# A planner's table of matmul durations is set to the spacings seen in the trace, and all operations are ordered anew

## The chip, the core and the metric

The kernel runs on one core of a Trainium2 chip. The metric is the device time of one execution in microseconds. A core has five engines that run side by side: PE (TensorE, the matrix engine, whose weight loads are listed apart as PEld), DVE (VectorE), ACT (ScalarE), POOL (GpSimd) and SP (SyncE, which issues the DMA transfers of this kernel). Each engine takes its own instructions in the order of the program, and waits where one of them needs a result of another engine or of a transfer.

## What is computed

One layer of a hybrid decoder, for a prompt of 512 tokens and for 8 samples of one token each, with D = 1024 and shared weights. The 512 + 8 = 520 tokens go through the products together. Cut to what matters:

```
mod = silu(c) @ w_ada + b_ada             # shift, scale, gate, twice
h = rmsnorm(x) * (1 + scale) + shift
proj = h @ w_in                           # u | z | xBC | dt | g_a | g_b
ya = S5(u)                                # 64 groups x 64 complex states, scan over time, gelu, half-GLU
yb = SSD(z, conv(xBC), dt)                # 32 heads of 64, d_state 128, chunks of 128 tokens
merged = sigmoid(g_a) * (ya @ w_branch_s5) + sigmoid(g_b) * (yb @ w_branch_ssd)
x += gate * rmsnorm(merged @ w_out)
x += gate_f * rmsnorm(swiglu(modulate(rmsnorm(x)) @ w_ffn_in) @ w_ffn_out)
```

The outputs are x for both groups and the new states: S5, SSD and convolution, for the prompt and for each sample.

## The kernel before, in words

Features lie on partitions, tokens along the free axis, in two halves of 260. All large products run as three matmuls with fp32r operands: weight and input are each split into a high and a low part, and high x high, high x low and low x high are summed (`product`, line 1148). For one block of 128 features by 128 and two halves of tokens that makes six matmuls of 260 columns, which are one operation of the **main stream**. The weights come in tiles of 512 KB by DMA; ACT makes their high part (`whi`, line 696) and DVE the low part (`wlo`, line 640). A finished tile in a PSUM bank pair (`pm`) is evacuated by ACT or DVE.

Beside the main stream run **side works**, written as generators: the modulation from `w_as` and `w_ada`, the eight S5 units (`s5_prep`, `s5_load`, `s5_body`, whose data go through DRAM as `ud`, `kd` and `yd` to change their layout), sixteen SSD units (`ssd_unit`, which load a broadcast row `acd` each), the samples' outputs (`ssd_y`, from `in_ssmT`) and the samples' new states (`ssd_state`, line 2369). This last one is a loop of 32 steps over two buffers: a load of 256 KB (`in_ssm`), three DVE operations on 512 columns, a store of 256 KB (`out_ssm_s`); the next load into a buffer waits for its store. Small matmuls of side works write to single banks (`bank`).

The order of all this is not written by hand. Every helper (`vtt`, `act`, `dma`, `mm`, ...) only records an operation, with the memory that it touches and an estimate of its duration, and a planner orders the records:

- While recording, `add` (line 240) gives each operation a time at once. `main` (line 755) moves the clock `now` on by the cost of a main product, and `tick` (line 823) lets side works record as much as fits before `now`. Memory is given out in this pass too.
- `order` (line 275) gives each operation a priority: for the main stream a running sum of its costs times `MAINF` = 1.1 (line 287), for side works the longest way to a main product or to the end. Then `play` (line 352) runs a course in which each engine takes the most urgent operation that can start, and `back` (line 315) derives new priorities from that course played backwards. This repeats 7 times, and then 24 times more with some priorities shifted at random (`SEED` = 149), three courses each. The course whose planned end is earliest becomes the program: the instructions of each engine in that order.
- `play` and `back` take the duration of an operation from the estimate of its helper, and the delay between engines from a table `DELAY` (line 179). For a transfer `dma` (line 698) takes 0.475 us (or 0.65) for the issue, 0.65 us, the bytes at 360 GB/s, and `DELAY` then adds 0.907 us to a reader on DVE; the transfers of the first weights, of `in_w_as` and of x have fixed urgencies from 1999 downward. The estimates for DVE are `.068 + columns / 960` us for two tensors (line 640), for ACT `.052 + columns / 1200` and a little more.

The planner acts when the program is built, not on the chip. Lines of the rows below are those of the helpers: L722 is every matmul of `mm`, L734 every transpose of `tp`, L729 the matmuls on zeros, L640 `vtt`, L696 `acp`, L691 `act`, L712 the DMA issue.

Of the kernel before, what the change touches and what calls it, by code (L numbers as in the profile page):

```python
# [49 lines left out]
class Root:  # L50
    """A tile: `get` gives the real one (it may be made late); `loc` names the memory it lies in."""
# [14 lines left out]
class Ap:  # L66
    """A view of a tile: its shape and addresses at once, the real view when the operation is issued."""
# [65 lines left out]
    def cells(self):  # L133
        """Partitions, and the set of words in one of them (bits of an integer)."""
        if self.root.bank:
            return 0, 128, 1
        p0, col = divmod(self.off, PSTEP)
        pn, run, outer = 1, 1, []
        for s, n in sorted(self.dims):
            if s >= PSTEP:  # L140
                pn = n
            elif s and n > 1:
                if s <= run:
                    run += s * (n - 1)
                else:
                    outer.append((s, n))
        m = (1 << run) - 1
        for s, n in outer:
            b = m
            for i in range(1, n):  # L150
                m |= b << (i * s)
        return p0, p0 + pn, m << col


def fold(dims):
    """The dimensions with neighbours joined where one stride serves both."""
    out = []
    for s, n in reversed(dims):
        if out and s == out[0][0] * out[0][1]:
            out[0] = (out[0][0], n * out[0][1])  # L160
        else:
            out.insert(0, (s, n))
    return out
# [14 lines left out]
# delay in us from the end of an operation to the start of one that waits for it  # L178
# [7 lines left out]
class Line:  # L186
    """The time of one engine: busy stretches, into whose gaps operations are put."""
# [24 lines left out]
class Plan:  # L212
    """Records operations with the memory they touch, and orders them for the engines."""
# [51 lines left out]
    def remake(self, loc, fn, words):  # L265
        """The memory `loc` gets a new tile: after everything that used the old one."""
        h = self.hist.get(loc, [])
        deps = {e[4]: .2 for e in h}
        o = Op("X", 0.0, fn, deps, None, 0.0)
        o.n = len(self.ops)  # L270
        self.ops.append(o)
        o.start = o.fin = max((p.fin for p in deps), default=0.0)
        self.hist[loc] = [[0, 128, (1 << words) - 1, True, o]]

    def order(self):
        """The best of some schedules: by the longest way to the end, then by latest starts."""
# [6 lines left out]
        after = 0.0  # L283
# [31 lines left out]
    def back(self):  # L315
        """Priorities from the schedule played backwards: the time from an operation's latest start to the end."""
# [35 lines left out]
    def play(self):  # L352
        """The course of the operations, each engine taking the most urgent of those that can start."""
# [69 lines left out]
    def shift(self, t, free, cand):  # L423
        """An operation of DVE that ACT may take at time t, where that is done sooner."""
# [32 lines left out]
class Arena:  # L457
    """One run of words in a tile of one type; blocks are cut out of it first fit."""
# [39 lines left out]
class Mem:  # L498
    """A fixed float32 arena, and slots whose type (float32 or float32r) is chosen when one is empty."""
# [10 lines left out]
    def find(self, n, dt, top):  # L510
        """The place for n words: an arena index (0 = the fixed one), or None."""
        if n > SLOT or (top or self.low and dt == F32) and self.a0.fit(n):
            return 0 if self.a0.fit(n) else None
        part = [(s.words(), i) for i, s in enumerate(self.slots) if self.mode[i] == dt and s.fit(n)]
        if part:
            return min(part)[1] + 1
        if dt == F32 and self.a0.fit(n) and n < 1500:
            return 0
        for i in range(NSLOT):
            if self.mode[i] is None:  # L520
                return i + 1
        if dt == F32 and self.a0.fit(n):
            return 0
        return None
# [76 lines left out]
class Builder:  # L601
# [76 lines left out]
    def relu(self, o, a, s):  # L678
        """max(a + s, 0)"""
# [18 lines left out]
    def dma(self, o, a, boost=0.0):  # L698
        """Starts a transfer; returns the estimate of its end."""
# [16 lines left out]
    def mm(self, o, l, r, start=True, stop=True):  # L716
        n, m = self.fs(r), l.shape[-1]
        if l.dtype == F32R:
            c = max(n / 2400, .111) if m > 32 else .048
        else:  # L720
            c = max(n * 4 / 2400, .216) * max(m, 32) / 128 + (.021 if m <= 64 else 0.0)
# [3 lines left out]
    def idle(self, o, n, after=None):  # L725
        """Matmuls on zeros."""
# [5 lines left out]
    def tp(self, o, a, n):  # L732
        d = self.ident[:n, :n]
        self.pe(.108, lambda: self.nc.tensor.transpose(real(o), real(a), real(d)), [o], [a, d])  # L734
# [8 lines left out]
    def bunch(self):  # L743
        """Matmuls that have to follow one another (sums that are open in one bank)."""
# [10 lines left out]
    def main(self):  # L755
        """The matmuls gathered in `group`, as one operation of the main stream."""
# [24 lines left out]
    def can(self, sizes, dt=F32, spare=0):  # L781
        """Whether the blocks fit, with room for `spare` token rows beside them."""
# [13 lines left out]
    def wblk(self, sizes, spare=2, dt=F32, prio=2):  # L796
        """Blocks for side work; a request that waits holds back those of less urgent work."""
# [88 lines left out]
    def ahead(self, j, table, f):  # L886
        """Prepares the weights of the use j of a chunk, unless that is done."""
# [12 lines left out]
    def build(self):  # L900
# [27 lines left out]
        # weight stream  # L928
# [30 lines left out]
        # half of the tokens at a time where the next step waits for all features  # L959
# [15 lines left out]
        # startup: modulation for the mixer, first norm  # L975
# [36 lines left out]
        # the first three tiles advance with the scale, two feature blocks at a time  # L1012
        b23 = [self.banks.pop() for _ in range(2)]
        ps = [[self.pm[0][:, n] for n in both], [self.pm[1][:, n] for n in both], b23]
        if NDUM:
            # matmuls on zeros: they keep the array busy, and so its clock at the full rate, until there are data
# [127 lines left out]
    def span(self, n):  # L1144
        """The tokens of half n."""
        return slice(n * self.cutp, n * T + (1 - n) * self.cutp)

    def product(self, hi, lo, k, p, halves, start, stop, xh, xl):
        """One block of features in a tile of the main stream."""
# [11 lines left out]
    def dt_mm(self, k, p, w):  # L1161
        """The 32 columns of dt, high and low parts side by side, summed later."""
# [50 lines left out]
    def scaled(self, k):  # L1213
        """hi/lo of the scaled input, a feature block: not yet normalized, and without the shift."""
# [11 lines left out]
    def evac_u(self, i, p):  # L1226
        """A tile of u made from the scaled input: normalized here."""
# [6 lines left out]
    def shift(self, gens):  # L1234
        """The shift; what it adds to the tiles of u that were made without it."""
# [31 lines left out]
    def turn(self, p, ev, n, md):  # L1267
        """Sums the four parts of sums in p, feature to partition."""
# [12 lines left out]
    def shifted(self, k):  # L1281
        """hi/lo of the normalized, scaled and shifted input."""
# [13 lines left out]
    def ada_s(self, k):  # L1296
        """The scale of the mixer's input, a feature block."""
# [52 lines left out]
    def ada_last(self):  # L1350
        """The gate of the second branch, in small pieces: needed much later, so it fills gaps."""
# [24 lines left out]
    def evac(self, kind, i, p, halves):  # L1376
# [9 lines left out]
        elif kind == "dt":  # L1386
            # the weights' high and low parts; later a chunk (and two samples) of a head a partition
# [136 lines left out]
    def cols(ap, halves):  # L1524
        """The tokens of the halves."""
# [35 lines left out]
    def mix_in(self, i, n, pv):  # L1561
        """A tile of the branch, times its gate and weight, and its squares, for half n of the tokens."""
# [58 lines left out]
    def finish(self, n):  # L1621
# [6 lines left out]
        for k in range(KD):  # L1628
            m, x, o = self.mixk(k)[:, c], self.xrk(k)[:, c], self.O["y"]
            self.vtt(m, m, rs, MULT)  # L1630
            if k < len(xp):
                # this sum on the tensor engine
# [12 lines left out]
    def rstd_last(self):  # L1645
        """The reciprocal deviations of the last 256 tokens: made with a token a partition, then spread by matmuls."""
# [39 lines left out]
    def gated(self):  # L1686
        # squares, normalization and splits of the SSD branch
# [43 lines left out]
    def s5(self):  # L1731
# [45 lines left out]
        # f = (abar - 1) / lam  # L1777
# [18 lines left out]
        # unit rotation by 8 angles  # L1796
# [30 lines left out]
        # powers in falling order, for B: the steps of a chunk that are left after a token  # L1827
# [39 lines left out]
    def ring(self, key, q, n, sizes):  # L1867
        """Blocks of the n-deep ring `key` for unit q; taken when first needed."""
# [10 lines left out]
    def s5_tabs(self, unit):  # L1879
        """cos and (signed) sin of 8 c theta, c = 0 .. 63, for the 8 groups of a unit, by doubling."""  # L1880
# [4 lines left out]
        for q in range(0, 8, 2):  # L1885
            w, pb = yield from self.ring("tw", 0, 1, [512, 1536])
            # planes: -sin, cos, sin; 64 partitions for each of the two units
# [35 lines left out]
    def s5_prep(self, q, un, KP, BB32):  # L1923
# [14 lines left out]
        # f B and, in bb's first plane, its copy; f B with its parts exchanged  # L1938
# [54 lines left out]
    def s5_load(self, q, un, U, Hm):  # L1993
# [18 lines left out]
        # decay of a chunk; the step of the samples' states  # L2012
# [81 lines left out]
    def ssd(self):  # L2094
# [25 lines left out]
        # dt = softplus(raw + bias)  # L2120
# [32 lines left out]
        # minus the sums of a; decay to chunk end times dt  # L2153
# [45 lines left out]
    def ssd_group(self, g, acd, act, dtT, ddT):  # L2199
        BT, CT = self.bt[g].v(T), self.ct_[g].v(T)  # L2200
        bs_, Bs, CB = yield from self.wblk([128, 512, 512], 0, F32, 1)
        # the samples: rows of B, columns of C, products for their dot products
# [44 lines left out]
    def ssd_unit(self, m, bl, Bs, CB, CT, acd, act, dtT, ddT, end):  # L2247
        """Two heads (one tile of 128 features): chunk states, recurrence over chunks, output, gate."""
# [72 lines left out]
    def ssd_y(self):  # L2321
        """The samples' outputs: C on the decayed old states (n on the partitions here), C B on what the new token adds."""
# [46 lines left out]
    def ssd_state(self):  # L2369
        """The samples' new states, a feature a partition."""  # L2370
# [31 lines left out]
def layout(inputs):  # L2402
# [18 lines left out]
    # S5 features: channel before group within a tile  # L2421
# [82 lines left out]
```

## Time and profile before

| | |
|---|---|
| time, three runs | 1200.11, 1202.06, 1204.35 us; median 1202.06 us |
| profiled execution | span 1193.2 us from the first to the last instruction; its own time is recorded by that span alone, 8.9 us below the median |
| PE busy | 1168.8 us, 98% of the span, 10,182 matmuls |
| PEld busy | 1124.5 us, 94% |
| DVE busy | 814.7 us, 68% |
| ACT busy | 576.3 us, 48% |
| DMA | 195.49 MB, 164 GB/s on average |
| granted TensorE clock | 0.998 of full speed on average |

Busy time of an engine is the union of its instructions. Matmuls overlap in the pipeline: one of 260 columns is shown with about 283 ns while the next one starts some 120 ns after it, so that the time per matmul is read from how many start in a stretch and not from the duration of one. A stretch without idle time of PE is one where no stop shows in its stream.

### The profile page before, as it was taken

Reading aid. Unit: us, or ns where it says so; the run is one execution under the profiler, and the core shown is the slowest. Engines: PE = TensorE matmul, PEld = TensorE weight load, DVE = VectorE, ACT = ScalarE, POOL = GpSimd, SP = SyncE. Lnnn points to the kernel's source line nnn. Section 1 sums busy time; section 2 is a strip of 40 time slices with the busy share of each in tenths; the row PEclk is TensorE's granted clock in tenths of the full one; section 3 lists DMA queues with packets and bytes.
Section 4 is the critical chain, followed back from the end, with each engine's and each line's share of the span. In section 5 each row is a group of like instructions: output and inputs, shape, how many; then the busy total and the mean of one; then the engine's idle time right before and its main releaser. Section 6 shows DMA issues by size and latency. Waiting matters only on the chain.

```text
span 1193.2 us, 24814 instructions
## 1 busy us (share of the span) xinstructions
PE 1168.8 (98%) x10182; PEld 1124.5 (94%) x10182; DVE 814.7 (68%) x1651; ACT 576.3 (48%) x981; POOL 4.9 (0%) x32
## 2 busy tenths in 40 slices
PE   8999999999999999999999999999999899999998
PEld 6899898999999999999998989999999899999997
DVE  6898989997696877868885435499576673322236
ACT  6655444357487657847853323465223222222233
POOL 0000000000000000000000000000000000000000
PEclk9999999999999999999999999999999999999999
DMA  8838698667243343355545674344566663223244
GB/s 292 278 119 219 162 215 224 180 160 208 82 134 101 114 128 125 116 175 169 188 145 201 241 268 144 129 166 147 182 217 203 198 206 104 88 81 97 83 130 135
DMA packets 118066, 195.49 MB, mean 164 GB/s; under 512 B 45856, under 2 KB 68800, under 8 KB 115648
## 3 DMA queue, kind: packets, MB, share of 16 engines
q1 hardware_dynamic: 117952, 193.90, 52.9%
q8 instruction: 80, 1.31, 0.4%
q14 instruction: 34, 0.28, 0.1%
HBM read 165.81 MB, written 23.86 MB: 159 GB/s over the span
## 4 chain that ended last, share of the span: by engine, by line
PE 79%; DMA 9%; DVE 7%; issue 1%; SPq 1%; ACT 1%; DVEq 0%; ACTq 0%
PE pm L722 64%; PE bank L722 14%; DVE s L640 4%; DMA arena<-in_ssm 3%; DVE arena L640 2%; PE bank L734 2%; DMA s<-in_w_as 1%; DMA out_ssm_s<-arena 1%; SPq L712 1%; DVE wlo L640 1%; DMA s<-in_w_in 1%; DMA ud<-s 1%; DMA s<-s 1%; DVE s L663 1%; ACT s L696 0%
## 5 line engine op out<-in xcount | busy, mean ns | idle before, releaser
L722 PE MATMUL pm<-hi,whi 128*128 128x260 f32 (+1 forms) x1856 | 497.5, 289 | 5.9 <-DVE arena L640 3.7
L722 PE MATMUL pm<-lo,whi 128*128 128x260 f32 (+1 forms) x1856 | 483.4, 282 | 0.0
L722 PE MATMUL pm<-hi,wlo 128*128 128x260 f32 x1840 | 370.4, 283 | 0.0
L722 PEld LDWEIGHTS pm<-hi,whi 128*128 128x128 f32 (+1 forms) x1856 | 349.6, 188 | 17.4 <-issue 13.0
L722 PEld LDWEIGHTS pm<-lo,whi 128*128 128x128 f32 (+1 forms) x1856 | 349.1, 188 | 0.1
L640 DVE TENSOR_TENSOR wlo<-arena,whi 128x1024 fp32r<-128x1024 f32 (+1 forms) x157 | 188.8, 1203 | 146.7 <-ACT whi L696 144.9
L722 PEld LDWEIGHTS pm<-hi,wlo 128*128 128x128 f32 x1840 | 282.9, 188 | 0.0
L696 ACT CAST whi<-arena 128x1024 fp32r<-128x1024 f32 (+1 forms) x158 | 162.6, 1029 | 197.1 <-PE pm L722 180.2
L722 PE MATMUL pm<-s,whi 128*128 128x260 f32 (+2 forms) x1128 | 184.2, 283 | 0.0
L640 DVE TENSOR_TENSOR arena<-arena 128x512 f32<-128x512 f32 (+11 forms) x299 | 140.3, 494 | 49.8 <-DMA arena<-in_ssm 29.4
L722 PEld LDWEIGHTS pm<-s,whi 128*128 128x128 f32 x1128 | 156.2, 188 | 5.1 <-issue 4.2
L722 PE MATMUL pm<-s,wlo 128*128 128x260 f32 (+2 forms) x564 | 117.2, 283 | 0.0
L722 PEld LDWEIGHTS pm<-s,wlo 128*128 128x128 f32 x564 | 88.1, 188 | 0.0
L691 ACT ACT_TABLE_LOAD x63 | 80.8, 1283 | 10.3 <-DMA s<-acd 3.5
L722 PE MATMUL bank<-s,s 128*64 128x128 f32 (+5 forms) x672 | 75.8, 282 | 5.6 <-ACT s L696 4.4
L722 PEld LDWEIGHTS bank<-s,s 128*128 128x128 f32 (+2 forms) x672 | 61.3, 164 | 10.9 <-ACT s L696 5.3
L691 ACT ACTIVATE s<-s 128x520 f32<-128x520 f32 (+10 forms) x89 | 50.0, 570 | 38.3 <-DVE s L640 17.7
L691 ACT ACTIVATE arena<-pm 128x260 f32<-128x260 f32 (+3 forms) x44 | 21.2, 489 | 92.7 <-PE pm L722 85.7
L640 DVE TENSOR_TENSOR s<-arena,s 128x520 fp32r<-128x520 f32 (+5 forms) x60 | 56.5, 948 | 10.6 <-ACT s L696 10.4
L640 DVE TENSOR_TENSOR s<-s,arena 128x8 f32<-128x8 f32 (+6 forms) x138 | 48.6, 369 | 13.8 <-ACT s L691 12.7
L722 PE MATMUL bank<-hi,s 128*128 128x260 f32 x256 | 55.5, 285 | 0.0
L722 PE MATMUL pm<-hi,s 128*128 128x260 f32 x256 | 55.0, 285 | 0.0
(122 smaller groups left out, 1265.8 us busy)
## 6 DMA issues: line engine op xcount, KB each, us to landing
arena<-in_w_in SPq DMA_DIRECT2D x59, 512.0 KB, 3.7
arena<-in_w_fi SPq DMA_DIRECT2D x44, 512.0 KB, 4.4
arena<-in_w_ada SPq DMA_DIRECT2D x12, 1024.0 KB, 7.5
arena<-in_w_fo SPq DMA_DIRECT2D x20, 512.0 KB, 3.6
arena<-in_ssmT SPq DMA_DIRECT2D x16, 512.0 KB, 4.4
s<-acd SPq DMA_DIRECT2D x16, 512.0 KB, 4.3
arena<-in_w_bssd SPq DMA_DIRECT2D x16, 512.0 KB, 5.4
arena<-in_ssm SPq DMA_DIRECT2D x32, 256.0 KB, 3.8
```

Of the source, the lines that this page charges most:

```text
L640: self.op("V", .068 + self.fs(o) / 960, lambda: self.nc.vector.tensor_tensor(out=real(o), in0=real(a), in1=real(b), op=op), [o], [a, b, *a ...
L663: self.op("V", .068 + self.fs(o) / 960, lambda: self.nc.vector.tensor_tensor_scan(out=real(o), data0=real(a), data1=real(b), initial=0.0, ...
L691: self.op("A", c, lambda: self.nc.scalar.activation(real(o), real(a), f, bias=real(bias), scale=real(scale)), [o], [a, scale, bias], None ...
L696: self.op("A", c, lambda: self.nc.scalar.copy(real(o), real(a)), [o], [a])
L712: p = self.op("S", .475 if same else .65, lambda: self.nc.sync.dma_start(out=real(o), in_=real(a)), [o], [a], None, c)
L722: self.pe(c, lambda: self.nc.tensor.matmul(real(o), lhsT=real(l), rhs=real(r), start=start, stop=stop), [o], [l, r])
L734: self.pe(.108, lambda: self.nc.tensor.transpose(real(o), real(a), real(d)), [o], [a, d])
```

## The change

Three estimates of PE's durations get other values, in microseconds; n is the number of columns of the moving operand, m that of the stationary one. Comments and docstrings go as well, which leaves blank lines (the line numbers stay). Nothing else differs in the file, but as the planner orders by these numbers, the recording, the use of memory and the order of all engines can come out different.

```diff
     def mm(self, o, l, r, start=True, stop=True):
         n, m = self.fs(r), l.shape[-1]
         if l.dtype == F32R:
-            c = max(n / 2400, .111) if m > 32 else .048
+            c = max(n / 2400 + (.0114 if n < 300 else .0025), .112)
         else:
-            c = max(n * 4 / 2400, .216) * max(m, 32) / 128 + (.021 if m <= 64 else 0.0)
+            c = max(n * 4 / 2400 + .005, .224) * max(m, 32) / 128 + (.021 if m <= 64 else 0.0)
...
     def tp(self, o, a, n):
         d = self.ident[:n, :n]
-        self.pe(.108, lambda: self.nc.tensor.transpose(real(o), real(a), real(d)), [o], [a, d])
+        self.pe(.112, lambda: self.nc.tensor.transpose(real(o), real(a), real(d)), [o], [a, d])
```

## Rows read from the trace of the kernel before

**Rows 1.** The page: the span, and engines with busy us, share and instructions.

```profile
span 1193.2 us, 24814 instructions
...
PE 1168.8 (98%) x10182; PEld 1124.5 (94%) x10182; DVE 814.7 (68%) x1651; ACT 576.3 (48%) x981; POOL 4.9 (0%) x32
```

**Rows 2.** Stretches: start to end, length, busy us per engine, clock, DMA share, GB/s.

```profile
0.00:42.00 42.00, 35.62 (x332) 28.69 (x333) 26.32 (x96) 25.73 (x63) 1.59 (x11) 1.00 0.92 328
...
90.00:245.00 155.00, 145.94 (x1274) 142.27 (x1273) 139.37 (x286) 72.35 (x172) 1.70 (x15) 0.99 0.80 198
245.00:600.00 355.00, 355.00 (x3328) 343.24 (x3327) 282.88 (x626) 246.19 (x350) 0.39 (x1) 1.00 0.46 141
...
845.00:955.00 110.00, 105.87 (x884) 105.48 (x883) 74.72 (x102) 28.83 (x37) 0.00 (x0) 1.00 0.63 201
955.00:1158.00 203.00, 203.00 (x1695) 203.00 (x1694) 73.60 (x93) 56.38 (x88) 0.00 (x0) 1.00 0.36 111
1158.00:1193.20 35.20, 30.36 (x232) 28.51 (x230) 20.75 (x44) 14.00 (x26) 0.00 (x0) 0.98 0.46 144
```

**Rows 3.** Chain by line: 0 to 60, 90 to 245, 245 to 600, 810 to 890, 890 to 956.

```profile
by line: PE pm L722 34.7%; DMA s<-in_w_as 26.8%; DMA s<-in_w_in 15.6%; SPq L712 8.7%; PE bank L722 7.5%; PE bank L734 1.8%; ACT whi L696 1.7%; issue 1.4%; ACT s L696 0.8%; ACTq L696 0.0%
...
by line: DVE s L640 26.0%; issue 7.1%; PE pm L722 6.5%; DVE wlo L640 6.1%; DVE arena L640 6.0%; DMA ud<-s 5.5%; DMA s<-s 5.1%; SPq L712 4.7%; DVE s L663 4.1%; ACT s L696 3.3%; DMA s<-in_s5m 3.3%; DMA s<-ud 3.0%; DMA acd<-s 2.8%; DMA arena<-
...
by line: PE pm L722 78.2%; PE bank L722 18.6%; PE bank L734 3.2%
...
by line: PE pm L722 77.0%; PE bank L722 22.6%; PE bank L734 0.5%
...
by line: DMA arena<-in_ssm 45.9%; DMA out_ssm_s<-arena 20.9%; DVE arena L640 16.0%; issue 7.5%; DVE wlo L640 3.9%; PE pm L722 2.4%; DVE s L640 2.2%; SPq L712 1.6%
```

**Rows 4.** Groups of instructions by form, PE: count | busy us, mean ns | idle before.

```profile
L722 PE MATMUL pm<-hi,whi 128*128 128x260 f32 x1840 | 493.7, 289 | 5.9 <-DVE arena L640 3.7 <-ACT s L691 1.0 <-ACT s L696 0.8
L722 PE MATMUL pm<-lo,whi 128*128 128x260 f32 x1840 | 479.6, 282 | 0.0
L722 PE MATMUL pm<-hi,wlo 128*128 128x260 f32 x1840 | 370.4, 283 | 0.0
```

**Rows 5.** Waits (us, times, longest), three of 60 to 270, two of 270 to 600.

```profile
ACT s L696 <- DMA ud<-s: 15.2, 6, 6.0
...
ACT s L696 <- DMA s<-s: 11.0, 9, 4.4
ACT s L691 <- DMA s<-in_s5hy: 6.5, 3, 3.1
...
ACT L691 <- DMA s<-acd: 3.5, 1, 3.5
...
DVE s L682 <- DMA s<-acd: 3.1, 4, 1.2
```

**Rows 6.** Tile in_ssm: loads with first and last issue, who waited, us to landing.

```profile
L712 SPq DMA_DIRECT2D arena<-in_ssm x32: 327/333/457, 813.4 to 973.1; - x32
...
  DVE arena L640: 29.4, 16
...
DMA to landing us min/median/max: 2.5/3.8/5.8
```

**Rows 7.** DMA issues: count, KB each, median us to landing.

```profile
s<-acd SPq DMA_DIRECT2D x16, 512.0 KB, 4.3
...
out_ssm_s<-arena SPq DMA_DIRECT2D x32, 256.0 KB, 3.0
```

**Rows 8.** Stretches as in rows 2: the state loop in two parts; 120 to 150.

```profile
813.40:890.00 76.60, 76.60 (x638) 75.39 (x637) 56.61 (x100) 24.02 (x41) 0.00 (x0) 1.00 0.61 196
890.00:956.00 66.00, 61.87 (x515) 61.48 (x515) 44.34 (x60) 17.41 (x22) 0.00 (x0) 1.00 0.64 204
...
120.00:150.00 30.00, 27.12 (x229) 26.41 (x228) 27.50 (x55) 13.77 (x32) 0.23 (x2) 0.94 0.66 161
```

**Rows 9.** Waits over the whole span: us, times, longest.

```profile
ACT whi L696 <- PE pm L722: 180.2, 59, 6.9
```

## The prediction

> **What bounds the kernel now.** I read the page's list of engines first, to see whether one of them fills the span. It does: PE is busy for 1168.8 of 1193.2 us, so only 24.4 us of the span have no matmul in flight [rows 1]. The change moves instructions and neither adds nor removes one, so the 10,182 matmuls stay, and all that it can move is those idle 24.4 us, in either direction.
>
> Then I read the table of stretches to see where the idle time lies, by subtracting PE's busy time from each stretch [rows 2]. It is 6.4 us in the first 42 us, 9.1 us between 90 and 245 us, 4.1 us between 845 and 955 us and 4.8 us after 1158 us; the other four stretches have none.
>
> The chain of waits, cut to stretches, then says what sets the pace in each [rows 3]. From 245 to 600 us and from 810 to 890 us it is PE alone. From 90 to 245 us (the S5 units) PE has 6.5% of it under its main line, and DVE, DMA and ACT have most of the rest. From 890 to 956 us (the samples' SSD states) the loads and stores of the state loop hold 66.8% (45.9 + 20.9) and PE 2.4%. So there are two places where work beside PE is already the slower partner, and both end in stalls of PE.
>
> **What the change does to the plan.** The planner orders by a table. For a product with 260 token columns the old table says 260/2400 = 108.3 ns, the new one 119.7 ns, a factor of 1.105. The chip agrees with the new one: between 955 and 1158 us PE runs 1,695 matmuls, nearly all of that form, in 203.00 us, 119.8 ns each [rows 2]. Three groups of this form alone hold 3 x 1840 = 5,520 of the 10,182 matmuls [rows 4]; at 11.4 ns each they add 63 us to the planned PE time. The durations of DVE, ACT and DMA in the table stay. On the chip PE takes what it took; what changes is how much PE work the plan lays beside a given amount of other work.
>
> That is the step on which the forecast rests. The old plan believed that 108.3 ns of other work fit beside one matmul, and the chip gave it 119.8 ns. So each stretch of other work had about 10% more time on the chip than planned, and late transfers were swallowed by that. The new plan lays only as many matmuls beside it as really fit. Because every engine takes its queue in the planned order, PE then meets a matmul whose input is late earlier than before.
>
> **The terms.** *PE's own work:* 10,182 matmuls before and after, 0 us.
>
> *Start and end:* in the first 60 us loads of w_as hold 26.8% of the chain and those of w_in 15.6% [rows 3]; they are the first transfers issued, by fixed urgencies (1999, then 1990 less their place) that no table touches, so I take 0 for the 6.4 us. The 4.8 us at the end are the last sums and their output, which nothing else can cover: 0 us.
>
> *The S5 stretch, 90 to 245 us:* the chip lays 145.9 us of PE beside this work [rows 2], and the old plan thought of it as 145.9 / 1.105 = 132.1 us. If the new plan lays 132.1 us of real PE time there and the work takes its present 155 us, PE idles 22.9 us, 13.8 us more than now. If the work shrinks to DVE's busy 139.4 us [rows 2], PE idles 7.3 us, 1.8 us less. The lowest end is that all 9.1 us go. Between -1.8 and +13.8 I take a point a third of the way up, +3.4 us: DVE is busy for 90% of the stretch, so that end is the nearer one, but ACT's waits for transfers (15.2 us for ud, 11.0 for s, 6.5 for s5hy between 60 and 270 us) [rows 5] are waits that no table of PE removes.
>
> *The state loop, 813 to 973 us:* 32 loads are issued from 813.4 to 973.1 us, one every 5.15 us, and DVE waits for 16 of them, 29.4 us in all; a load lands 3.8 us after its issue [rows 6], a store 3.0 us after [rows 7]. The planner's formula for a load of 256 KB (line 698: 0.475 for the issue, 0.65, 262144/360e3 = 0.73, and 0.907 to the reader) makes 2.76 us, about 1 us short. From 890 to 956 us, where the loop sets the pace, 61.9 us of PE lie beside it [rows 8]; the new plan lays 61.9 / 1.105 = 56.0 us there, and if the loop can't be quicker PE idles 10.0 us in place of 4.1, +5.9 us. From 813 to 890 us PE sets the pace and could lose up to 76.6 - 76.6 / 1.105 = 7.3 us if 5.15 us a load is the loop's own limit there too [rows 8], and nothing if it isn't. The lowest end is -4.1, the present stall gone. I take half of 5.9, +3.0 us, since half of the loads are waited for.
>
> For the transfer at the root of this term the Trainium skill, DMA: Bandwidth & Descriptors, section Anatomy of one DMA, gives about 2.0 us fixed plus the bytes at 436 GB/s (a fit for DMAs issued by GpSimd), 2.6 us for 256 KB as an estimate; by that the planner's 2.76 us would be long enough, this term would be 0 and the sum 3.4 us. The trace does not agree: its median is 3.8 us, and the term stands.
>
> *Stretches without idle time, 245 to 845 and 955 to 1158 us:* PE covers all the rest there, so 0 us; what it costs if that cover is gone is the last rival.
>
> *The clock:* one stall in the S5 stretch let the granted clock fall from the 2.4 to the 1.2 GHz level, 0.94 on average from 120 to 150 us [rows 8], which is 0.06 x 30 = 1.8 us of PE time. One more such fall is in the range, not in the sum.
>
> Sum: 0 + 3.4 + 3.0 = +6.4 us. The profiled execution has a span of 1193.2 us, and the median of the three runs, 1202.06 us, is 8.9 us above it for what lies around; I leave that as it is: 1193.2 + 6.4 + 8.9 = **1208.5 us**.
>
> **The rivals.** *Faster: the right table removes the stalls.* Where the old plan expects PE too early, ACT and DVE stand before an evacuation or a free buffer while other work lies behind it in their queues: ACT's split of weights alone waits 180.2 us for PE [rows 9]. An order with the right times fills that, and the S5 work and the loop come earlier. It decides if the transfers named above have work in front of them in the new order. At most the two inner stalls go, 9.1 + 4.1 = 13.2 us; two thirds of that give 1193.3 us. Against it: an ACT that waits for PE marks a place where PE is late, and there PE has no idle time to win.
>
> *No difference.* PE is busy for 98% and every order issues the same matmuls; the first pass of the planner already multiplies main products by MAINF = 1.1, which makes 119.2 ns of 108.3. Then the shuffling of orders (24 perturbations, best by the planner's own end) trades one small stall for another: 1202 us within 3.6. Against it: MAINF stands in the first priorities alone; the course that is played and its reversal use the table's value. Those 3.6 us, 0.3%, are about what a measurement of this kernel can tell from no change.
>
> *Slower in a new place: the SSD units lose their cover.* From 245 to 600 us PE never idles [rows 2], but 16 units each begin with a load of acd that lands after 4.3 us [rows 7], where the planner's formula makes 3.5 us for 512 KB. If each unit's first matmul stands where the plan says, PE waits 0.8 us 16 times, 12.8 us: with the two terms above 1221.3 us, alone 1214.9 us. Against it: DVE has 72 us to spare there [rows 2], and only 3.5 + 3.1 us of waits for acd show on any engine [rows 5].
>
> **How the numbers follow.** The forecast, the lost cover in the two known places, has 0.40. The SSD units' stall has 0.15, no difference 0.21, the removed stalls 0.24. The ends of the terms are 1202.1 - 13.2 = 1188.9 and, with 13.8 + 5.9 + 7.3 + 1.8 = 28.8, 1230.9 us. Leaving out a tenth at each side, the range is 1195 to 1224 us. Faster by over 0.3% has 0.24, within it 0.21, slower 0.55 (0.40 + 0.15). As most of the chance lies on one side, the forecast's own range is 1204 to 1222 us.
>
> **What would show it.** Right: PE idle between 90 and 245 us (or where the S5 units then end) near 12.5 us, and in the state loop near 7 us; the loop's 32 loads in fewer than 160 us of PE work, with DVE's wait for them above 29.4 us; other stretches still without idle time; the same 119.8 ns a matmul. Wrong: less PE idle than 24.4 us in all, which is the first rival; or idle time between 245 and 600 us behind acd or ssmT, which is the last. If the clock falls below 1.00 in more slices than now, the size is wrong and not the mechanism. If the matmul count or the spacing moved, the premise would be wrong.

## The result, and the profile after

The changed kernel takes 1214.74 us (median of 4 runs, 1210.26 to 1218.05) against 1201.09 us before (4 runs, 1198.45 to 1204.35): a ratio of 1.0117, 95% interval 1.0088 to 1.0146. It is slower by 13.7 us; 6.4 us were forecast (1208.5 us, range 1195 to 1224).

The page of the changed kernel, its span and its engines:

```profile
span 1211.3 us, 24833 instructions
...
PE 1181.6 (98%) x10182; PEld 1132.3 (93%) x10182; DVE 811.0 (67%) x1631; ACT 573.3 (47%) x997; POOL 4.7 (0%) x32
```

As many matmuls as in [rows 1], and PE is still busy for 98%. Its idle time is 1211.3 - 1181.6 = 29.7 us where it was 24.4 us, and its busy time has grown by 12.8 us with nothing more to do.

Two stretches hold the two places of the prediction in both kernels, whose events moved by up to 18 us: 60 to 330 us (the S5 units) and 800 to 1020 us (the state loop). The table of stretches has start to end, length, busy us (and instructions) of PE, PEld, DVE, ACT and POOL, the granted clock, DMA share and GB/s. First the kernel before:

```profile
60.00:330.00 270.00, 260.94 (x2299) 254.56 (x2299) 236.86 (x513) 137.69 (x296) 2.94 (x20) 0.99 0.67 174
...
800.00:1020.00 220.00, 215.87 (x1794) 213.23 (x1793) 145.75 (x232) 66.54 (x99) 0.00 (x0) 1.00 0.55 175
```

and the changed one, with its stretch between them and the main products at the end as in [rows 2]:

```profile
60.00:330.00 270.00, 258.12 (x2229) 251.85 (x2228) 230.00 (x501) 133.58 (x288) 2.74 (x19) 0.97 0.66 171
330.00:800.00 470.00, 469.46 (x4209) 438.25 (x4208) 316.01 (x646) 270.28 (x409) 0.32 (x1) 1.00 0.48 158
800.00:1020.00 220.00, 213.33 (x1745) 212.27 (x1744) 154.95 (x256) 74.45 (x119) 0.00 (x0) 0.98 0.55 173
...
955.00:1158.00 203.00, 203.00 (x1694) 203.00 (x1693) 74.10 (x93) 54.69 (x83) 0.00 (x0) 1.00 0.37 112
```

PE's idle time grows from 9.1 to 11.9 us in the first place and from 4.1 to 6.7 us in the second, and between them it stays near zero (0.5 of 470 us). The spacing of the last main products is the same, 203.00 us for 1,694 matmuls.

How such a stall comes about, seen on DVE and PE in the state loop (timeline of the changed kernel: start, us, instruction, and in brackets the idle time before it with what ended it):

```profile
942.12 1.22 DVE L640 TENSOR_TENSOR wlo<-arena,whi 128x1024 fp32r<-128x1024 f32 x1
947.13 1.42 DVE L640 TENSOR_TENSOR arena<-arena 128x512 f32<-128x512 f32 x2 [3.79 <-DMA arena<-in_ssm]
948.46 0.69 DVE L640 TENSOR_TENSOR arena<-arena,pm 128x520 f32<-128x520 f32 x1
...
949.30 0.56 PE L722 MATMUL pm<-hi,whi 128*128 128x260 f32 x1 [3.07 <-DVE arena L640]
949.65 0.42 PE L722 MATMUL pm<-lo,whi 128*128 128x260 f32 x1
949.87 0.42 PE L722 MATMUL pm<-hi,whi 128*128 128x260 f32 x1
```

DVE stands 3.79 us before a state whose load has not landed. Behind it in the queue is the evacuation of a PSUM tile (the third line), and PE waits 3.07 us for that bank. The matmuls after the stop start about 0.22 us apart and not 0.12: the granted clock was 0.50 from 949 to 955 us. In the S5 stretch a stop runs through ACT and DVE:

```profile
194.59 1.18 ACT L696 COPY s<-arena 128x512 f32<-128x512 f32 x1 [2.81 <-DMA ud<-s]
...
196.42 0.68 DVE L640 TENSOR_TENSOR s<-s 128x496 f32<-128x496 f32 x1 [2.20 <-ACT s L691]
...
198.99 0.35 ACT L691 ACTIVATE s<-s,arena 128x64 f32<-128x64 f32 x1 [2.31 <-DMA s<-in_s5hy]
201.03 0.41 ACT L691 ACTIVATE s<-s 128x248 f32<-128x248 f32 x1 [1.70 <-DVE s L640]
201.35 1.05 ACT L696 COPY s<-bank 128x512 f32<-128x512 f32 x2
...
202.46 1.34 PE L722 MATMUL bank<-s,s 128*128 128x72 f32 x5 [4.43 <-ACT s L696]
```

The copies at 201.35 make the operand of the matmul, and PE idles 4.43 us. Ahead of them on ACT stand two late transfers and a wait for DVE. DVE had itself waited for an activation that stands behind the late ud in ACT's queue, and then ran until 201.0 us, so the chain of this stop goes back to ud; in_s5hy was late too, but ACT would still have waited for DVE. Waits of the changed kernel that answer to [rows 6] and [rows 9] (us in total, times, longest):

```profile
ACT whi L696 <- PE pm L722: 165.5, 55, 5.5
...
DVE arena L640 <- DMA arena<-in_ssm: 41.4, 21, 3.9
```

DVE waits for the states 21 times where it was 16, 41.4 us where it was 29.4, while a load now lands after 3.5 us and not 3.8. The loads are not slower; DVE comes to them sooner.

### The profile page after: what moved, and what is told of

The parts are those of the page before. It is cut to its first block, busy times and chain, and to the rows that moved or that the text cites. A ratio compares the mean times of both kernels' runs of the same rounds, so it can differ in the third digit from the quotient of the medians.

```text
span 1211.3 us, 24833 instructions
## 1 busy us (share of the span) xinstructions
PE 1181.6 (98%) x10182; PEld 1132.3 (93%) x10182; DVE 811.0 (67%) x1631; ACT 573.3 (47%) x997; POOL 4.7 (0%) x32
## 4 chain that ended last, share of the span: by engine, by line
PE 66%; DVE 13%; DMA 13%; ACT 3%; issue 2%; SPq 2%; DVEq 0%; ACTq 0%
PE pm L722 54%; PE bank L722 10%; DVE s L640 4%; DVE arena L640 4%; DMA arena<-in_ssm 3%; DMA out_ssm_s<-arena 2%; DMA s<-in_w_as 2%; SPq L712 2%; DVE wlo L640 2%; PE bank L734 1%; DMA ud<-s 1%; DVE s L651 1%; ACT s L696 1%; DMA s<-in_w_in 1%; DMA s<-s 1%
## 5 line engine op out<-in xcount | busy, mean ns | idle before, releaser
L696 ACT CAST whi<-arena 128x1024 fp32r<-128x1024 f32 (+1 forms) x158 | 162.7, 1030 | 206.3 <-PE pm L722 165.5
L640 DVE TENSOR_TENSOR arena<-arena 128x512 f32<-128x512 f32 (+11 forms) x299 | 141.0, 494 | 70.5 <-DMA arena<-in_ssm 41.4
L722 PE MATMUL bank<-s,s 128*64 128x128 f32 (+5 forms) x680 | 78.3, 286 | 7.0 <-ACT s L696 6.5
L691 ACT ACTIVATE s<-s 128x520 f32<-128x520 f32 (+11 forms) x90 | 50.7, 571 | 48.8 <-DVE s L640 20.1
L640 DVE TENSOR_TENSOR s<-s,s 128x512 f32<-128x512 f32 (+9 forms) x90 | 54.9, 617 | 3.8 <-ACT s L691 3.2
L722 PE MATMUL bank<-hi,s 128*128 128x260 f32 x256 | 52.7, 286 | 1.4 <-ACT arena L691 1.4
L640 DVE TENSOR_TENSOR s<-s,arena 128x8 f32<-128x8 f32 (+6 forms) x129 | 43.0, 349 | 16.4 <-ACT s L691 11.8
```

The source lines that it names most:

```text
L640: self.op("V", .068 + self.fs(o) / 960, lambda: self.nc.vector.tensor_tensor(out=real(o), in0=real(a), in1=real(b), op=op), [o], [a, b, *a ...
L691: self.op("A", c, lambda: self.nc.scalar.activation(real(o), real(a), f, bias=real(bias), scale=real(scale)), [o], [a, scale, bias], None ...
L696: self.op("A", c, lambda: self.nc.scalar.copy(real(o), real(a)), [o], [a])
L722: self.pe(c, lambda: self.nc.tensor.matmul(real(o), lhsT=real(l), rhs=real(r), start=start, stop=stop), [o], [l, r])
```

## The experiments

All kernels were run beside the kernel before, whose medians in the three groups were 1204.62, 1204.15 and 1203.88 us. The runs are called e1 to e12. Ratios have the median of their group as base. They are made from all runs; the quotient of the two medians lies within 0.0015 of them, save for e9, where it is 1.0052 and not 1.0029. The changed kernel's 1.0117 has the four runs of its own group as base (1201.09 us); against these 53 later runs (median 1204.18 us) its 1214.74 us are 1.0088. The loss to be explained is thus 0.9 to 1.2%.

**Which pass of the planner counts.** The durations serve twice: while recording (pace of the side works, use of memory) and in the ordering. Each PE operation was given both costs; the recording took one, and just before the ordering the other was put in its place:

```diff
+        for o in self.plan.ops:
+            if o.eng == "P":
+                o.cost = o.later
         done, self.second = self.plan.order()
```

Old durations in the recording and new ones in the ordering:

> The old durations while recording (pacing of side works, memory), the new ones in the ordering. Lost cover in the ordering: as slow as the changed kernel, 1.008 to 1.015 of the kernel before, with single stalls of PE over 2 us in the S5 stretch or the state loop and a clock fall behind each. The recording is the cause: within 0.4% of the kernel before. A draw among orders: anything from 0.997 to 1.02.

Measured (e1): 1227.08 us, 1.0184 (1.0158 to 1.0209). Slower than either theory of a cause had it, and on the side of the ordering. Its waits of PE:

```profile
PE pm L726 <- DVE arena L640: 11.2, 6, 3.8
PE bank L726 <- ACT s L696: 7.8, 4, 5.2
PE pm L726 <- ACT s L696: 6.5, 4, 2.3
```

Line 726 is line 722 of the kernel before. The changed kernel has the same three waits, each with fewer stops and less time:

```profile
PE bank L722 <- ACT s L696: 7.4, 3, 4.4
PE pm L722 <- DVE arena L640: 5.2, 4, 3.1
...
PE pm L722 <- ACT s L696: 1.5, 1, 1.5
```

So in this order PE stops behind the same engines, more often.

The halves exchanged:

> The new durations while recording, the old ones in the ordering. Lost cover in the ordering: within 0.4% of the kernel before. The recording is the cause: 1.008 to 1.015. A draw among orders: anything from 0.997 to 1.02, and not what the run with the halves exchanged gives.

Measured (e2): 1204.43 us, 0.9997 (0.9982 to 1.0012). So the loss comes with the ordering by the new durations; the recording by them costs nothing. (The ordering uses the durations once more, in a rule of `play` at line 404 that doubles some of PE's; in the course chosen it acts only on operations of the plan's first 10 us, with either table, so it is not the cause.)

**A lucky draw?** The planner shifts priorities at random. With `SEED` at 150 and 151 in place of 149, old and new table each:

> The kernel before with other random shifts of the priorities. Lost cover: a draw with the old table, 0.995 to 1.006 of the kernel before. If the kernel before is a lucky draw and the table means nothing: 1.005 to 1.02, like the changed kernel.

Measured (e5): 1197.00 us, 0.9933 (0.9911 to 0.9955).

> The changed kernel with the same other shifts. Lost cover: slower than the old table with this seed by 0.5 to 2%, 1.005 to 1.02 of the kernel before, single stalls of PE over 2 us and clock falls again. A draw alone: no order between this one and the old table's.

Measured (e6): 1227.93 us, 1.0189 (1.0159 to 1.0219). The longest stops of PE are 6.5, 4.0 and 3.7 us.

> As with seed 150 on the old table: 0.995 to 1.006 by lost cover, 1.005 to 1.02 if the kernel before is a lucky draw.

Measured (e7): 1196.91 us, 0.9949 (0.9930 to 0.9968).

> As with seed 150 on the new table: 1.005 to 1.02 by lost cover and slower than the old table with seed 151; a draw alone: no order between the two tables.

Measured (e8): 1219.78 us, 1.0134 (1.0106 to 1.0163). The kernel before is, if anything, the worst of the three draws with its table, a little beyond what was expected on the good side, and the changed kernel the best of those with the new one. Of four orders made with the old durations (with the run of exchanged halves) none is slower than 1.000, of four made with the new ones none is faster than 1.012.

**Does the loss come from transfers that land late?** One microsecond more between every transfer and its reader in the planner's table:

```diff
-         ("S", "V"): .907, ("S", "A"): .908, ("S", "G"): .935, ("S", "P"): .98, ("S", "S"): .95}
+         ("S", "V"): 1.907, ("S", "A"): 1.908, ("S", "G"): 1.935, ("S", "P"): 1.980, ("S", "S"): 1.950}
```

On the changed kernel:

> The changed kernel, with the planner's delay from a transfer to its reader 1 us longer, which is what the landings in the trace lack. Lost cover: the stalls behind transfers go, PE idle falls from 29.7 to under 24 us and the clock falls with it, ratio 0.993 to 1.004. Not transfers: stays at 1.008 to 1.015. A draw: anything in 0.997 to 1.02.

Measured (e3): 1203.93 us, 0.9997 (0.9985 to 1.0008). The time returned, which a draw among orders could also have given; of the signs expected, only one of two places shows it, the second line:

```profile
60.00:330.00 270.00, 255.28 (x2193) 248.69 (x2192) 227.35 (x493) 134.22 (x286) 2.88 (x19) 0.98 0.66 168
...
800.00:1020.00 220.00, 219.73 (x1818) 216.95 (x1817) 157.09 (x252) 74.84 (x120) 0.00 (x0) 1.00 0.57 177
```

In the state loop PE's idle time falls from 6.7 to 0.3 us, but among the S5 units it is 14.7 us, above the 11.9 us of the changed kernel; in all it is 28.2 us and not under 24. So idle time is only 1.5 us of the 10.8 us between the medians of the two kernels. The mean clock of its runs was 0.994 where that of the changed kernel's was 0.990 (0.9905 before rounding), some 4 us more. The rest is not explained by these rows.

On the kernel before:

> The kernel before with the same 1 us on transfers. Lost cover: little to win, as the old table already gives that time, 0.995 to 1.003. A draw: anything in 0.997 to 1.02.

Measured (e4): 1192.69 us, 0.9898 (0.9875 to 0.9921), faster than either theory had it, and faster than both kernels. It is one order, and the old table gave 0.993 and 0.995 with other shifts alone. Its two stretches:

```profile
60.00:330.00 270.00, 261.97 (x2293) 255.62 (x2293) 240.74 (x511) 141.34 (x305) 3.24 (x21) 0.99 0.70 175
...
800.00:1020.00 220.00, 220.00 (x1813) 216.04 (x1812) 146.62 (x229) 67.42 (x102) 0.00 (x0) 1.00 0.56 174
```

The old table had too little time for transfers as well: 4.1 us of idle time in the loop are gone and 1.0 of the 9.1 us among the S5 units.

**The state loop alone.** The changed kernel with the 1 us on the transfers of `ssd_state` only:

```diff
-            return self.dma(h0s[n % 2], self.I["ssm"][g, b // 2][:, b % 2])
+            return self.dma(h0s[n % 2], self.I["ssm"][g, b // 2][:, b % 2], late=1.0)
...
-            self.dma(self.O["ssm_s"][g, b // 2][:, b % 2], h0)
+            self.dma(self.O["ssm_s"][g, b // 2][:, b % 2], h0, late=1.0)
```

(and the same for the load of `bcd`).

> The changed kernel with 1 us more for the transfers of the state loop alone. Lost cover in two places: PE idle and the clock fall between 890 and 960 us go, the S5 stretch keeps its stalls; a third to two thirds of the loss returns, 1.003 to 1.009 of the kernel before. If the loop costs nothing: 1.010 to 1.015.

Measured (e9): 1210.18 us, 1.0029 (1.0010 to 1.0048). By these ratios 0.0088 of the 0.0117 returned; by the medians alone (1.0052) it is 0.0065 of 0.0117, or 0.0036 of 0.0088 on the base of the 53 runs. Stretches, and the loop's loads with who waited for them:

```profile
60.00:330.00 270.00, 257.93 (x2165) 251.87 (x2164) 225.99 (x492) 131.22 (x284) 2.72 (x19) 0.94 0.65 169
...
800.00:1020.00 220.00, 218.57 (x1818) 218.17 (x1817) 163.32 (x272) 80.48 (x138) 0.00 (x0) 1.00 0.55 174
```

```profile
  DVE arena L642: 8.2, 5
```

DVE waits 8.2 us for the states in place of 41.4, PE idles 1.4 us in the loop's stretch in place of 6.7, and the S5 stretch keeps its 12.1 us, as lost cover in two places would have it. From the first load to the last store PE now runs 1536 matmuls beside the loop where it was 1260, and PE has no idle time left there:

```profile
834.70:1018.40 183.70, 183.70 (x1536) 183.70 (x1535) 128.58 (x194) 53.71 (x78) 0.00 (x0) 1.00 0.59 188
```

The share of the loss that returned is between two fifths and three quarters, by the base that is taken; the range written was a third to two thirds. The clock works against it: among the S5 units it was 0.94 in this execution and 0.97 in the changed kernel, with nearly the same idle time.

**More cover still.** Main products planned shorter than before, on the old table:

```diff
-            c = max(n / 2400, .111) if m > 32 else .048
+            c = max(n / 2640, .101) if m > 32 else .048
```

> The kernel before with the main products planned another 9% shorter (260/2640 = 98.5 ns): a table more wrong, with more cover. Lost cover: no slower than the kernel before, 0.988 to 1.002. If the old table was good because it was nearly right: slower, 1.003 or more.

Measured (e10): 1206.63 us, 1.0024 (1.0001 to 1.0047), between the two. The loop's stretch has 2.4 us of idle time and the S5 stretch 8.3 us, both below the kernel before, but 7.9 us stand before 60 us (6.4 before) and 2.4 us between 330 and 800 us (none before); in all PE idles 27.5 us, 3.1 us more than before. The two places are better covered, and the idle time has come up elsewhere.

Two microseconds more on every transfer, new table:

> The changed kernel with 2 us more on every transfer. Lost cover: between the 1 us version of the changed kernel and the 1 us version of the kernel before, 0.988 to 1.000. If 1 us was all that the transfers lacked: 0.997 to 1.005.

Measured (e11): 1199.01 us, 0.9945 (0.9930 to 0.9961), as expected, with 6.1 us of idle time among the S5 units and none in the loop. Old table:

> The kernel before with 2 us more on every transfer. Lost cover: near its floor already with 1 us, 0.985 to 0.995. If too much time planned for transfers costs as well: 0.995 to 1.005.

Measured (e12): 1206.31 us, 1.0010 (0.9997 to 1.0024). It fits that too much planned for transfers costs as well, though e4 and e12 are one order each and draws with one table differ by up to 0.7%: the S5 and loop stretches are as good as with the new table (6.2 and 0 us), but 3.7 us of idle time stand between 330 and 800 us, where the kernel before has none.

PE's idle time in the two stretches, all by the same subtraction (length less PE busy), and how long DVE waits for the states' loads, in us:

| kernel | ratio | 60 to 330 us | 800 to 1020 us | DVE's wait for in_ssm |
|---|---|---|---|---|
| before | 1 | 9.1 | 4.1 | 29.4 |
| order by old table: e2, e5, e7 | 0.9997, 0.9933, 0.9949 | 6.2, 9.7, 9.0 | 3.0, 0.4, 2.5 | 30.7, 34.8, 32.0 |
| changed | 1.0117 | 11.9 | 6.7 | 41.4 |
| order by new table: e1, e6, e8 | 1.0184, 1.0189, 1.0134 | 16.8, 17.9, 11.3 | 11.2, 7.8, 8.5 | 41.7, 40.8, 41.9 |

The means are 8.5 and 2.5 us with the old durations, 14.5 and 8.5 us with the new: 6 us more in each place. In no column do the orders by the old table and those by the new one overlap. The three orders by the new table with more time for transfers (e3, e9, e11: 0.9997, 1.0029, 0.9945) all lie below the four without (1.0117 to 1.0189).

## Why the prediction was right, and where it was not

**The sign held, and the mechanism in the state loop.** The recording does not matter (e2), other random shifts do not change the picture (e5 to e8), and time put back into the plan for transfers returns the loss (e3, e11) or part of it (e9, in the loop alone). The rival "faster" fell: ACT's wait for PE did shrink (165.5 from 180.2 us) and nothing was won by it. "No difference" fell with the intervals. The SSD units did not lose their cover: 0.5 us of idle time between 330 and 800 us. The prediction's sentence on the Trainium skill, DMA: Bandwidth & Descriptors, section Anatomy of one DMA, would have had the state loop cost nothing, as an estimate from a fit for DMAs issued by GpSimd. The trace does not agree: the loads land after 3.5 us in the changed kernel, and e9 shows that the loop did cost time.

**The state loop.** +3.0 us was the term, and PE's idle time in its stretch rose by 2.5 us (6.7 less 4.1, before rounding). The picture behind it held too, though less than 1.105-fold, and DVE's wait for the loads grew as foreseen (41.4 from 29.4 us). From the first load to the last store of the loop PE runs 1355 matmuls before and 1260 after, 7% fewer for the same 32 steps:

```profile
813.40:980.40 167.00, 162.87 (x1355) 161.26 (x1354) 120.09 (x186) 48.18 (x71) 0.00 (x0) 1.00 0.63 203
```

```profile
827.20:986.90 159.70, 154.47 (x1260) 153.75 (x1260) 114.58 (x180) 45.01 (x66) 0.00 (x0) 0.98 0.63 196
```

**The S5 stretch.** +3.4 us was the term and 2.8 us the rise of idle time, but its working fails, so that the agreement is luck. It had the new plan lay fewer matmuls beside the S5 work. From the first load of in_s5m to the store of the last S5 state the changed kernel runs 2561 matmuls and not 2471, and takes 15.9 us longer:

```profile
43.80:334.40 290.60, 281.54 (x2471) 273.58 (x2470) 256.64 (x550) 153.70 (x326) 2.94 (x20) 0.99 0.67 173
```

```profile
44.60:351.10 306.50, 294.62 (x2561) 286.21 (x2560) 264.82 (x571) 155.67 (x327) 2.85 (x20) 0.98 0.63 164
```

The stop followed above goes back to ud, one of the transfers that the term named. But ACT's waits for those transfers hardly grew (ud 16.1 from 15.2 us, s 12.4 from 11.0) or shrank (in_s5hy 2.8 from 6.5), and the one that grew was not named, the load of in_s5m; first the kernel before, then the changed one, 60 to 330 us:

```profile
ACT s L691 <- DMA s<-in_s5m: 3.6, 2, 2.0
```

```profile
ACT s L691 <- DMA s<-in_s5m: 15.6, 4, 4.1
```

No run shows how much of PE's idle time goes back to it. 1 us more on transfers did not lessen the idle time there (14.7 us in e3) and 2 us did (6.1 us in e11). What sets the length of this work in the plan stays open.

**The size.** The two terms together were +6.4 us, and the idle time of PE rose by 5.3 us; the time rose by 13.7 us. The step that failed is the sum's assumption that idle time is all that the change can move: the clock at 0, and nothing for delays that the profile doesn't count as idle. The prediction's own sign for this came: the clock is below 1.00 in more stretches than before. Two things are in the difference of the traces:

```profile
core 0: 1193.2 us, clock 0.998
```

```profile
core 0: 1211.3 us, clock 0.990
```

The first line is the kernel before, the second the changed one. A microsecond at the 1.2 GHz level loses half a microsecond, so span times the granted clock is the span without that loss: 1190.8 and 1199.2 us, 8.4 us apart in place of 18.1. The other 9.7 us of that pair are clock, at most: time at the low level in which PE had nothing to do is counted in them. Over runs this part is smaller, because the trace of before was an unusually quiet execution: 53 later ones of the same kernel lie between 1199.61 and 1208.03 us (median 1204.18) at clocks of 0.989 to 0.994. Taking run means, span times clock is 1192.3 us before and 1200.9 us after, +8.6 us, and the clock adds 0.9918 against 0.9905, some 1.6 us; that is +10.2 us against the 53 runs, and the remaining 3.5 us to 13.7 are the spread between the groups of runs of the kernel before. In the pair of traces PE's busy time rose by 12.8 us, of which at most 9.7 us are clock; at least 3.1 us are left that are neither idle nor clock. A matmul is listed with some 283 ns while the next follows after 120 ns, so each stop is counted about 160 ns short. But the lists of PE's waits name 19 stops before and 21 after, so two more make some 0.3 us; what the rest is stays open.

The 8.9 us that I put around the span were wrong in kind as well: in every run whose span is listed, the time is 1.7 to 2.4 us above the span. The other 7 us fit clock falls of the median execution that the profiled one did not have: as an estimate, 1190.8 us at the mean clock of 0.992 of the 53 later runs make a span of 1200.4 us and a time of 1202.4. This cancels in the sum, as it stands on both sides.

## What to carry to other kernels

In a static order an error in one estimate can be slack that covers an error in another; before one estimate is made right, see which other estimates lean on its error. Here the matmuls planned 10% too short gave cover to loads planned about 1 us too short: mending the first alone cost 0.9 to 1.9% in four orders, mending the second alone won 1.0% in the one order tried with 1 us, and mending both gave the time of before (e3). Try such a change with several seeds of the planner, since single draws with one table differed by 0.7%.

## What was not expected of the hardware

Executions of one kernel on one core differ by their clock falls: the kernel before ran at 0.998 in the profiled execution and at 0.989 to 0.994 in 53 others, some 7 us of its 1200, with the same instructions. So one trace can't tell how much a stall costs in falls of the clock. What follows a long stall can be seen: PE stood still for 4.43 us from 198 us on, and in the changed kernel the granted clock fell during that stop and stayed low behind it,

```profile
198.00:203.00 5.00, 0.56 (x4) 0.55 (x3) 4.90 (x10) 2.31 (x6) 0.00 (x0) 0.80 0.82 196
203.00:210.00 7.00, 7.00 (x42) 7.00 (x42) 6.90 (x12) 3.18 (x9) 0.00 (x0) 0.66 0.88 214
```

which is 0.34 x 7 = 2.4 us of PE time beside the 4.43 us. The part of the fall before 203 us cost little, as PE had no matmul to run for most of it. The slowest order (e6) had a clock of 0.984 in its profiled execution. The mean clock of runs was 0.993 over the four orders by the old durations and 0.988 over the four by the new: about 6 of the 22 us between their mean times. How much of the time goes with the clock is not fixed by the idle time alone: e9 has 1.4 us of idle time in the loop and 24.5 us in all, as much as the kernel before in its trace, and yet its runs had a mean clock of 0.987.
